# A decoder layer on one core: merge gates two ways, block sums in other buffers, and filler work placed by attention unit

## The chip, the core and the metric

The kernel runs on one core of one Trainium2 chip. A core has TensorE (PE, whose weight loads are listed as PEld), VectorE (DVE), ScalarE (ACT), GpSimd (POOL) and SyncE (SP), which here issues the transfers. Each engine works through its own list of instructions in order and waits at semaphores for the others. The metric is the device time of one execution in microseconds; every time in this document is in microseconds unless it is marked ns.

## What is computed

One layer with 1,024 tokens of 1,024 channels. The normed input is projected to everything that the three branches need, and to three merge gates of 1,024 channels each:

```python
xn = rms_norm(x, norm_mix)
proj = xn @ w_in        # NSA q, k/v, branch gates | conv GLU | memory q | 3 merge gates
br_nsa = nsa_attention(...) @ w_nsa_out    # compressed, selected, window; gated sum
br_conv = u @ w_conv_out                   # GLU, depthwise conv of 31 taps, LayerNorm, silu
br_mem = o_m @ w_mem_out                   # cross-attention into 256 memory tokens
gm = jax.nn.sigmoid(g_merge).reshape(b, s, N_BRANCH, D_MODEL)
merged = gm[:, :, 0] * br_nsa + gm[:, :, 1] * br_conv + gm[:, :, 2] * br_mem
h = x + merged @ w_out
hn = rms_norm(h, norm_ffn)
return h + (jax.nn.silu(hn @ w_gate) * (hn @ w_up)) @ w_down
```

## The kernel before

**Arithmetic.** All products keep float32 accuracy: each operand is split into a high part (a cast on ACT, `split`) and the low rest (a subtraction on DVE or POOL, `sub`), and `mm3` issues three matmuls, high by high, high by low and low by high. A matmul has 128 rows of weights and mostly 512 columns of tokens.

**Order of the program.** Norm and projections, the conv and memory branches and the attention's keys and values come first; then the attention, in 80 units (8 blocks of 128 queries, 2 groups, and for each a compressed unit, two selected and two window units); then the merge (branch projections, gated sums), the output projection, gate/up and down. A unit has a part `scores` (products, masks on DVE, exponentials on ACT, scales of the softmax on POOL in `softmax_tail`) and a part `values` (transposes, splits, products). `values` is issued LAG = 4 units behind its `scores`.

**The filler.** The merge gates are twelve pairs of 256 columns (`pairs`, in the order of the branches conv, memory, NSA). They depend on the normed input alone and are needed only in the merge, so they are put between other work: the instructions are written with a low priority (`low(FILL)`), and a scheduler, which picks the next instruction of each engine by priority among those that it deems ready, puts them into gaps. Their results go to one PSUM bank of their own (`fbank`, tile `pf`), their split weights to two buffers `fslab` (tile `fsl`), and they pass through DRAM (`zd`, `z1d`) to the merge.

A pair is 256 columns by 1,024 channels by 1,024 tokens, seen as two by two blocks. Before, all twelve go by seven half products in place of eight. Two of the seven use input blocks as they are (slabs 180 to 183 in the rows below): these are the *early* products, 24 matmuls a pair, with a load `fst` of 512 KB, a cast and a subtraction on POOL. The other five, 60 matmuls a pair, are the *late* products: four of them need sums of input blocks, of which three take the place of blocks in XN and one has slabs of its own, `T2`. So the block sums come behind the last early product that reads the old blocks. The sums use temporaries from `t4`, which the attention uses too. The late products need five weight operands, three of them with sums of weight blocks (`fs`, `wsx`, from a 512 KB load into the one buffer `wextra`): four sums on POOL, three of the five splits on POOL and two on DVE. Each result is added to a kept part on DVE (`put`, L882: tiles `fp`, `fz`). A list `spread` ties every late product to a point of the attention by an order-only dependency, in proportion to the work of the units.

**The merge** loads branch outputs and projection weights in 512 KB units, one weight unit for each two pairs' columns, reads the gates from `zd`, and multiplies.

Of the kernel before, what the change touches and what calls it, by code (L numbers as in the profile page):

```python
# [32 lines left out]
WB, LAG, SPREAD = 6, 4, 97  # L33
# [5 lines left out]
def hybrid_layer_kernel(  # L39
# [72 lines left out]
    def fbank(shape, dt=F32, p=P):  # L112
        return pfp.tile([p] + shape, dt, tag="pf", name=nm("pf"))
# [9 lines left out]
    class low:  # L123
        def __init__(self, by):
            self.by = by

        def __enter__(self):
            self.was = tc.cur_priority
            tc.cur_priority = self.was + self.by

# [125 lines left out]
    def unit(src, shape, alloc=wslab, eng=None, load=False):  # L256
# [4 lines left out]
        ld = nc.sync.dma_start(st, src)  # L261
        w = alloc([2] + shape)
        split(w[:, 0], w[:, 1], st, eng)
        return (w, ld.ins) if load else w

    def col_unit(w, c0, n=P, alloc=wslab, eng=None, load=False):
        return unit(w[:, c0:c0 + n].rearrange("(k p) c -> p k c", p=P), [w.shape[0] // P, n], alloc, eng,
                    load)
# [388 lines left out]
    with low(FILL):  # L657
        for n_, (b_, dp) in enumerate(pairs):
            w = col_unit(w_in, C_GM + b_ * D + 2 * dp * P, alloc=fslab, eng=nc.gpsimd)
            ps = fbank([512])  # L660
            for u in range(2):
                for k in range(4 * u, 4 * u + 4):
                    mm3(ps, w[:, 0, k, :], w[:, 1, k, :], xn(0, k, 0), xn(1, k, 0), k == 0, k % 4 == 3, True)
                z = fzp.tile([P, 512], F32, tag="fz", name=nm("fz"))
                nc.scalar.copy(z, ps)
                nc.sync.dma_start(zd[b_, 2 * dp, :, 0:512] if u else z1d[n_], z)

    T2 = [slab([2, 2, 512]) for _ in range(2)]
    for j in range(2):
        x11, x12, x22 = XN[0][j], XN[1][j], XN[1][2 + j]  # L670
        f = []
        for t in (x11, x12, x22):
            f.append(t4([2, 512]))
            nc.gpsimd.tensor_tensor(f[-1], t[:, 0].bitcast(F32), t[:, 1].bitcast(F32), op=OP.add)
        sub(nc.vector, f[1], f[1], f[0])
        split(x12[:, 0], x12[:, 1], f[1])
        sub(nc.vector, f[2], f[2], f[1])
        split(T2[j][:, 0], T2[j][:, 1], f[2])
    for sign, u in ((1, 0), (-1, 1)):
        for j in range(2):  # L680
            t, x_ = T2[j], XN[0][2 * u + j]
            d0, d1 = t4([2, 512]), t4([2, 512])
            for d, hl, eng in ((d0, 0, nc.vector), (d1, 1, nc.gpsimd)):
                a, b = (t, x_) if sign > 0 else (x_, t)
                sub(eng, d, a[:, hl].bitcast(F32), b[:, hl].bitcast(F32))
            nc.vector.tensor_tensor(d0, d0, d1, op=OP.add)
            split(x_[:, 0], x_[:, 1], d0)
# [79 lines left out]
    def values(u, tiles):  # L767
# [4 lines left out]
        if br == 0:  # L772
            b = bank([4, P], at=1)
            for h in range(4):
                nc.tensor.transpose(b[:64, h, :], tiles[h], ident)
            pt = t2([4, P], F32R)
            split(pt[:64], pt[64:], b[:64])
            m = mm(o.rearrange("p h q -> p (h q)"), vcmp[:, g, :], pt.rearrange("p h q -> p (h q)"), True, False)
            anchors.append((3, m.ins))
            return  # L780
# [18 lines left out]
        anchors.append((WB + nb, m.ins))  # L799
# [15 lines left out]
    load_q(0, 0)  # L815
    for u in units:
        if u[2] == 1 and u[3] == 1 and u[:2] != (NT - 1, 1):
# [4 lines left out]
    for u_ in ahead:  # L822
        values(*u_)


    late = len(pairs) * 20
    total = sum(w_ for w_, _ in anchors)
    spread, run = [], 0
    for w_, ins in anchors:
        run += w_  # L830
        while len(spread) < min(late, late * run * 100 // (total * SPREAD)):
            spread.append(ins)

    class fill_weights:
# [3 lines left out]
        def take(self, src, eng):  # L838
# [4 lines left out]
            split(w[:, 0], w[:, 1], src, eng)  # L843
            return w

    with low(FILL):
        fw, at_ = fill_weights(), [0]
        gp = nc.gpsimd

        def fill_product(ps, w, op, start):  # L850
            for k in range(4):
                first = mm3(ps, w[:, 0, k, :], w[:, 1, k, :], op(0, k), op(1, k), start and k == 0, k == 3, True)
                tc.add_manual_dep(first.ins, spread[at_[0]].name, ORDER, reason="spread over the attention")
                at_[0] += 1

        def blk(tiles):
            return lambda hl, k: tiles[k // 2][:, hl, k % 2, :]

        t1, t2_, t3_, t4_, x22 = blk(XN[1][:2]), blk(T2), blk(XN[0][:2]), blk(XN[0][2:]), blk(XN[1][2:])
        for n_, (b_, dp) in enumerate(pairs):  # L860
            r = wextra([2, KT, P], F32)
            for c in range(2):
                c0 = C_GM + b_ * D + (2 * dp + c) * P
                nc.sync.dma_start(r[:, c], w_in[:, c0:c0 + P].rearrange("(k p) c -> p k c", p=P))
            A11, A12, A21, A22 = r[:, 0, 0:4], r[:, 0, 4:8], r[:, 1, 0:4], r[:, 1, 4:8]
            sc = fzp.tile([P, 4, P], F32, tag="fz", name=nm("fs"))
            z1 = fzp.tile([P, 512], F32, tag="fz", name=nm("fz"))
            nc.sync.dma_start(z1, z1d[n_])
            pq = fstp.tile([P, 2, 512], F32, tag="fst", name=nm("fp"))
            p15, c12 = pq[:, 0], pq[:, 1]  # L870
            gp.tensor_tensor(sc, A21, A22, op=OP.add)
            s1 = fw.take(sc, gp)
            sub(gp, sc, sc, A11)
            sub(gp, A12, A12, sc)
            s4 = fw.take(A12, nc.vector)
            s2 = fw.take(sc, gp)
            sub(gp, A11, A11, A21)
            s3 = fw.take(A11, nc.vector)
            a22 = fw.take(A22, gp)

            def put(o, ps, z):
                nc.vector.tensor_tensor(o, ps, z, op=OP.add)  # L882

            ps = fbank([512])
            fill_product(ps, s1, t1, True)
            put(p15, ps, z1)
            fill_product(ps, s4, x22, False)
            put(c12, ps, z1)
            ps = fbank([512])
            fill_product(ps, s2, t2_, True)  # L890
            put(c12, ps, c12)
            nc.sync.dma_start(zd[b_, 2 * dp, :, 512:], c12)
            fill_product(ps, s3, t3_, False)
            put(p15, ps, p15)
            nc.sync.dma_start(zd[b_, 2 * dp + 1, :, 512:], p15)
            fill_product(ps, a22, t4_, False)
            put(z1, ps, z1)
            nc.sync.dma_start(zd[b_, 2 * dp + 1, :, 0:512], z1)
# [383 lines left out]
```

## Time and profile before

| | before |
|---|---|
| device time, median of 3 runs | 1787.79 |
| lowest and highest of the 3 | 1784.71, 1789.56 |
| the profiled execution's own time | 1791.22 |
| its span, first to last instruction | 1789.5 |
| PE busy | 1698.7 (95%) |
| DVE, ACT, POOL busy | 1146.3 (64%), 752.3 (42%), 747.3 (42%) |
| mean granted PE clock over the span | 0.981 |

Busy shares are of the whole span, which has stages with different limits. The granted clock is a share of the full TensorE clock, 2.4 GHz; 1.2 GHz would be 0.5, and a stretch between the two had some time at either level. The profiled execution is 3.43 above the median of the three runs; sums below are made in its time.

### The profile page before, as it was taken

Reading aid. Unit: us, or ns where it says so; the run is one execution under the profiler, and the core shown is the slowest. Engines: PE = TensorE matmul, PEld = TensorE weight load, DVE = VectorE, ACT = ScalarE, POOL = GpSimd, SP = SyncE. Lnnn points to the kernel's source line nnn. Section 1 sums busy time; section 2 is a strip of 40 time slices with the busy share of each in tenths; the row PEclk is TensorE's granted clock in tenths of the full one; section 3 lists DMA queues with packets and bytes.
Section 4 is the critical chain, followed back from the end, with each engine's and each line's share of the span. In section 5 each row is a group of like instructions: output and inputs, shape, how many; then the busy total and the mean of one; then the engine's idle time right before and its main releaser. Section 6 shows DMA issues by size and latency. Waiting matters only on the chain. (4 is left out here: it accounts for less than half of the span.)

```text
span 1789.5 us, 25276 instructions
## 1 busy us (share of the span) xinstructions
PE 1698.7 (95%) x9339; PEld 1467.7 (82%) x9339; DVE 1146.3 (64%) x1839; ACT 752.3 (42%) x1412; POOL 747.3 (42%) x605
## 2 busy tenths in 40 slices
PE   7999798999699999999779999999999999999999
PEld 5887787999588888998667899888888888888887
DVE  5499998766877788787343641775445455457665
ACT  5312444444476666766323432552222222224432
POOL 1102575575665555664222420055555776510000
PEclk9999899999799999999999999999999999999999
DMA  6212342222223222123635622233323444795663
GB/s 203 73 32 89 130 135 84 65 90 100 72 81 88 71 71 66 57 66 114 198 120 167 207 66 83 112 104 97 112 83 106 164 136 153 238 394 184 210 240 121
DMA packets 213463, 222.96 MB, mean 125 GB/s; under 512 B 28439, under 2 KB 157751, under 8 KB 212315
## 3 DMA queue, kind: packets, MB, share of 16 engines
q1 hardware_dynamic: 213338, 221.35, 38.0%
q8 instruction: 73, 1.20, 0.3%
q14 instruction: 52, 0.42, 0.1%
HBM read 165.73 MB, written 55.57 MB: 124 GB/s over the span
## 5 line engine op out<-in xcount | busy, mean ns | idle before, releaser
L151 PE MATMUL pf<-slab,fsl 128*128 128x512 f32 x1092 | 291.3, 407 | 28.3 <-ACT fsl L138 16.0
L151 PEld LDWEIGHTS pf<-slab,fsl 128*128 128x128 f32 x1092 | 202.7, 194 | 73.3 <-ACT fsl L138 19.0
L151 PE MATMUL ps<-slab,wsl 128*128 128x512 f32 (+1 forms) x1068 | 239.3, 381 | 3.0 <-DVE t L135 2.4
L151 PEld LDWEIGHTS ps<-slab,wsl 128*128 128x128 f32 x1068 | 194.0, 189 | 41.9 <-issue 2.6
L377 DVE SCALAR_TENSOR_TENSOR slab<-slab,cw 128x1019 f32<-128x1019 f32 (+18 forms) x120 | 188.6, 1581 | 1.8
L151 PE MATMUL ps<-wsl,slab 128*128 128x256 f32 x1224 | 165.1, 288 | 3.3 <-POOL wsl L135 1.6
L1112 DVE TENSOR_TENSOR t<-ps,t 128x512 f32<-128x512 f32 x127 | 86.9, 688 | 115.1 <-PE ps L151 114.0
L151 PEld LDWEIGHTS ps<-wsl,slab 128*128 128x128 f32 x1224 | 156.0, 195 | 5.6 <-POOL wsl L135 1.9
L151 PE MATMUL ps<-slab,fsl 128*128 128x512 f32 x636 | 147.7, 389 | 0.0
L151 PEld LDWEIGHTS ps<-slab,fsl 128*128 128x128 f32 x636 | 119.4, 188 | 24.8
L151 PE MATMUL ps<-slab,wsx 128*128 128x512 f32 (+1 forms) x596 | 136.5, 383 | 0.2 <-ACT wsx L138 0.2
L135 DVE TENSOR_TENSOR t<-ps,t 128x512 fp32r<-128x512 f32 (+3 forms) x196 | 121.1, 630 | 21.6 <-ACT t L138 20.1
L151 PEld LDWEIGHTS ps<-slab,wsx 128*128 128x128 f32 x596 | 109.5, 188 | 22.5 <-ACT wsx L138 0.6
L151 PE MATMUL ps<-t,slab 128*128 128x256 f32 x624 | 120.1, 298 | 2.4 <-DVE t L135 2.0
L138 ACT CAST t<-ps 128x512 fp32r<-128x512 f32 (+2 forms) x192 | 98.0, 540 | 48.5 <-PE ps L791 44.2
L151 PEld LDWEIGHTS ps<-t,slab 128*128 128x128 f32 x624 | 96.1, 194 | 10.3 <-DVE t L135 3.2
L151 PE MATMUL ps<-slab,qt 128*128 128x384 f32 (+3 forms) x384 | 100.5, 353 | 3.6 <-DVE sm L759 3.3
L1125 POOL TENSOR_TENSOR t<-t,t 128x512 f32<-128x512 f32 x21 | 39.2, 1865 | 116.9 <-DVE t L1112 42.4
L1077 POOL TENSOR_TENSOR t<-st 128x512 f32<-128x512 f32 x21 | 27.4, 1303 | 139.6 <-DVE slab L135 112.6
L929 POOL TENSOR_TENSOR slab<-slab,t 128x512 f32<-128x512 f32 x32 | 44.0, 1392 | 93.0 <-DVE t L928 87.3
L1216 PE MATMUL ps<-wsl 128*128 128x512 f32 x336 | 81.2, 389 | 0.0
L1216 PE MATMUL ps<-fsl 128*128 128x512 f32 x330 | 79.8, 389 | 0.0
(264 smaller groups left out, 3381.1 us busy)
## 6 DMA issues: line engine op xcount, KB each, us to landing
t<-in_w_down_dram SPq DMA_DIRECT2D x70, 256.0 KB, 3.9
wsx<-in_w_in_dram SPq DMA_DIRECT2D x24, 512.0 KB, 5.1
t<-zd SPq DMA_DIRECT2D x24, 512.0 KB, 4.1
st<-in_w_in_dram SPq DMA_DIRECT2D x22, 512.0 KB, 3.7
st<-in_w_gate_dram SPq DMA_DIRECT2D x22, 512.0 KB, 4.0
st<-in_w_up_dram SPq DMA_DIRECT2D x22, 512.0 KB, 4.0
ad<-t SPq DMA_DIRECT2D x44, 256.0 KB, 2.9
ads<-slab SPq DMA_DIRECT2D x33, 256.0 KB, 2.9
```

The lines of the kernel that those rows point to most:

```text
L135: eng.tensor_tensor(o, a, b, op=OP.subtract)
L138: nc.scalar.copy(hi, src)
L151: m = nc.tensor.matmul(o, a, b, start=start, stop=stop, skip_group_check=chain)
L377: return nc.vector.scalar_tensor_tensor(acc[:, s:], u[:, :S - s], cw[:, ct, 30 - s:31 - s], acc[:, s:], op0=OP.mult, op1=OP.add)
L929: nc.gpsimd.tensor_tensor(a, a, z, op=OP.add)
L1077: gp.tensor_tensor(s12[:, 0], u[:, 0], u[:, 1], op=OP.add)
L1112: nc.vector.tensor_tensor(o, a_, b_, op=OP.add)
L1125: nc.gpsimd.tensor_tensor(u4, u4, c22, op=OP.mult)
L1216: nc.tensor.matmul(B[t], a_, b_, start=start and k == 0 and j == 0, stop=k == FH - 1 and j == 2, skip_group_check=True)
```

## The change

The first two pairs (N_PLAIN = 2) are computed plainly: eight half products of 12 matmuls, all of them early, in four groups, with two `fst` loads a pair; the other ten stay with seven. The early products of the last four pairs (N_DUE = 4) are written at normal priority. The block sums are restated as `block_sub`: two differences (high on DVE, low on POOL), an addition on DVE, a cast on ACT and a subtraction on DVE, eight times; their temporaries come from `wextra` (four) and from `fslab` (four), in place of `t4`. All five weight splits of a late pair are on POOL. Late products get the priority of the attention unit that they are due with (`at(steps[...])`), spread over the units FILL_FROM = 4 to FILL_TO = 82 by weight, and each pair's weights that of eight units earlier (FILL_LEAD); the order-only dependency is now to the `values` of the unit LAG before.

```diff
-WB, LAG, SPREAD = 6, 4, 97
+WB, LAG = 6, 4
+FILL_LEAD, FILL_FROM, FILL_TO = 8, 4, 82
+N_PLAIN, N_DUE = 2, 4
...
-    with low(FILL):
-        for n_, (b_, dp) in enumerate(pairs):
-            w = col_unit(w_in, C_GM + b_ * D + 2 * dp * P, alloc=fslab, eng=nc.gpsimd)
-            ps = fbank([512])
-            for u in range(2):
...
+    for n_ in range(NP):
+        with low(FILL if n_ < NP - N_DUE else 0):
+            for c in range(2 if n_ < N_PLAIN else 1):
+                st = fstp.tile([P, KT, P], F32, tag="fst", name=nm("fst"))
+                nc.sync.dma_start(st, gate_columns(n_, c))
+                w = fslab([2, KT, P])
+                split(w[:, 0], w[:, 1], st, gp)
+                for half in range(2 if n_ < N_PLAIN else 1):
+                    ps = fbank([512])
+                    for u in range(2):
+                        half_product(ps, w[:, :, 4 * u:4 * u + 4], blk((x12, x22)[u] if half else (x11, x21)[u]), u == 0)
+                        if u or n_ >= N_PLAIN:
+                            z = f512("fz")
+                            nc.scalar.copy(z, ps)
+                            nc.sync.dma_start(gate_out(n_, c, half) if u else z1d[n_], z)
...
+    def block_sub(o, a, b, temps):
+        d = temps([2, 2, 512], F32)
+        for hl, eng in ((0, nc.vector), (1, gp)):
+            sub(eng, d[:, hl], a[:, hl].bitcast(F32), b[:, hl].bitcast(F32))
+        nc.vector.tensor_tensor(d[:, 0], d[:, 0], d[:, 1], op=OP.add)
+        split(o[:, 0], o[:, 1], d[:, 0])
+
     for j in range(2):
...
-            f.append(t4([2, 512]))
-            nc.gpsimd.tensor_tensor(f[-1], t[:, 0].bitcast(F32), t[:, 1].bitcast(F32), op=OP.add)
...
+        block_sub(x12[j], x12[j], x11[j], wextra)
+        block_sub(T2[j], x22[j], x12[j], wextra)
+    for j in range(2):
+        block_sub(x11[j], T2[j], x11[j], fslab)
+    for j in range(2):
+        block_sub(x21[j], x21[j], T2[j], fslab)
...
-        while len(spread) < min(late, late * run * 100 // (total * SPREAD)):
-            spread.append(ins)
...
-            s4 = fw.take(A12, nc.vector)
...
-            s3 = fw.take(A11, nc.vector)
...
+        while len(due) < (NP - N_PLAIN) * 20 * run // total:
+            due.append(k_)
...
+        with at(step_of(j_, -FILL_LEAD)):
+            r = wextra([2, KT, P], F32)
...
+                u_ = due[j_ + 4 * q + k]
+                with at(steps[min(u_ + 1, len(steps) - 1)]):
+                    m = mm3(ps, ws[q][:, 0, k, :], ws[q][:, 1, k, :], op(0, k), op(1, k), start and k == 0, k == 3, True)
+                    if u_ >= LAG:
+                        tc.add_manual_dep(m.ins, anchors[u_ - LAG].name, ORDER, reason="spread over the attention")
```

**Instructions in all.** On PE the filler has 24 matmuls of 128x512 more (1,116 in place of 1,092 with `slab` and `fsl` operands). DVE has 30 fewer (the 24 subtractions of late weights gone, 10 fewer `put`, 4 more of 128x1024 in the block sums), POOL 6 more (18 more late weight splits, 8 fewer weight sums, 2 more early splits, 4 fewer others of the late weights, 2 fewer in the block sums), SP 6 fewer.

**PE at the start of the attention.** In rows of the order a name is tile<-weights,moving operand, then the shape and the count; `pf` rows are filler, those with slabs 180 to 183 early products, `identr` rows the transposes of the last keys, `L716` (now `L752`) the first queries, `kcmp` rows the scores of a compressed unit, `L791` (now `L827`) transposes of `values`. Before:

```order
L151 MATMUL pf_4159<-slab_180,fsl_4156 128x512 x6
L151 MATMUL pf_4159<-slab_181,fsl_4156 128x512 x6
L637 MATMUL ps_3746<-identr,t_471_3670 128x128 x4
L151 MATMUL pf_4159<-slab_182,fsl_4156 128x512 x6
L151 MATMUL pf_4159<-slab_183,fsl_4156 128x512 x6
L637 MATMUL ps_3752<-identr,t_479_3741 128x128 x4
L716 MATMUL ps_4247<-ident,t_558_4244 128x128 x4
L151 MATMUL ps_4257<-kcmp,qt_4252 128x64
```

All early products are over when the attention's first scores begin. After the change, at the same place:

```order
L164 MATMUL pf_4115<-slab_183,fsl_4112 128x512 x6
L649 MATMUL ps_3752<-identr,t_479_3741 128x128 x4
L752 MATMUL ps_4415<-ident,t_566_4412 128x128 x4
L164 MATMUL pf_4151<-slab_180,fsl_4148 128x512 x6
L164 MATMUL pf_4151<-slab_181,fsl_4148 128x512 x6
L164 MATMUL ps_4425<-kcmp,qt_4420 128x64
```

Six early pairs more (pf_4151, pf_4187, pf_4223, pf_4259, pf_4295, pf_4331, 144 matmuls) now stand between the scores and values of the first sixteen units. The last of them, and what follows to the first late product (pf_8294):

```order
L164 MATMUL pf_4331<-slab_182,fsl_4328 128x512 x6
L164 MATMUL pf_4331<-slab_183,fsl_4328 128x512 x6
L164 MATMUL ps_4811<-t_711_4917,slab_3169 128x256
L164 MATMUL ps_4931<-slab_3166,qt_4855 128x256 x2
L164 MATMUL ps_4811<-t_711_4917,slab_3169 128x256 x3
L827 MATMUL ps_4945<-ident,wsl_4821 128x128 x4
L164 MATMUL ps_4936<-slab_3166,qt_4855 128x256 x2
L164 MATMUL ps_4966<-slab_3167,qt_4855 128x256 x2
L164 MATMUL ps_4811<-t_719_4946,slab_3169 128x256
L811 MATMUL ps_4981<-ident,t_699_4869 64x128 x4
L164 MATMUL ps_4811<-t_719_4946,slab_3169 128x256 x3
L164 MATMUL ps_4971<-slab_3167,qt_4855 128x256 x2
```

Between the last early product and the first late one there is now attention work alone.

**DVE in that stretch.** `fsl_4394` and `fsl_4400` are temporaries of block sums (L148 the subtractions, L713 the addition, `slab_180` to `slab_183` the blocks), `t_711` and `t_719` the splits of the attention's transposed probabilities that the PE rows above read, `L795` the masks of the scores. After the change:

```order
L148 TENSOR_TENSOR t_711_4917<-ps_4916,t_711_4917 128x512
L713 TENSOR_TENSOR fsl_4394<-fsl_4394 128x1024
L732 RECIPROCAL sm_4878<-sm_4859 128x4
L795 ISA wsl_4896,sm_4897<-ps_4899,strip 128x256
L795 ISA sm_4897 128x1
L795 ISA wsl_4896,sm_4897<-ps_4904,strip 128x256
L148 TENSOR_TENSOR fsl_4400<-slab_182,slab_4362 128x1024
L148 TENSOR_TENSOR slab_181<-fsl_4394,slab_181 128x1024
L148 TENSOR_TENSOR t_719_4946<-ps_4945,t_719_4946 128x512
L713 TENSOR_TENSOR fsl_4400<-fsl_4400 128x1024
```

The block sums of the first two slabs of XN stand between the splits of the attention's units; before, they stood ahead of the attention.

**PE behind the attention.** `wsl` and `wsx` rows are the merge's first and second weight unit, `pf` rows filler (slabs 321 to 324 are the rewritten blocks). Before:

```order
L151 MATMUL ps_9270<-slab_9245,wsl_9250 128x512 x3
L151 MATMUL pf_8994<-slab_182,fsl_8962 128x512
L151 MATMUL pf_8994<-slab_183,fsl_8962 128x512 x6
L151 MATMUL pf_9061<-slab_321,fsl_9045 128x512 x6
L151 MATMUL pf_9061<-slab_322,fsl_9045 128x512 x6
L151 MATMUL pf_9061<-slab_323,fsl_9045 128x512 x6
L151 MATMUL pf_9061<-slab_324,fsl_9045 128x512 x6
L151 MATMUL pf_9088<-slab_4190,fsl_9052 128x512 x6
L151 MATMUL pf_9088<-slab_4191,fsl_9052 128x512 x6
```

This block goes on with pf_9088 and pf_9154; then six matmuls of the second weight unit (wsx_9317) follow, and 36 filler matmuls of pf_9181 behind them. After the change:

```order
L164 MATMUL ps_9251<-slab_9226,wsl_9231 128x512 x3
L164 MATMUL ps_9304<-slab_9211,wsx_9298 128x512 x2
L164 MATMUL ps_9318<-slab_9211,wsx_9298 128x512 x2
L164 MATMUL ps_9304<-slab_9211,wsx_9298 128x512
L164 MATMUL ps_9304<-slab_9216,wsx_9298 128x512 x3
L164 MATMUL ps_9304<-slab_9221,wsx_9298 128x512 x3
L164 MATMUL pf_9162<-slab_4362,fsl_9124 128x512 x6
L164 MATMUL pf_9162<-slab_4363,fsl_9124 128x512 x6
```

The merge's second weight unit follows the first directly, and 48 late matmuls of the last pair stand in pieces of 12 among merge rows, in place of the block.

## Rows read from the trace of the kernel before

**Rows 1.** The page's first part (busy, share of the span, instructions) and its slices of 44.7 us each: PE's busy tenths, its granted clock in tenths, and GB/s moved.

```profile
PE 1698.7 (95%) x9339; PEld 1467.7 (82%) x9339; DVE 1146.3 (64%) x1839; ACT 752.3 (42%) x1412; POOL 747.3 (42%) x605
...
PE   7999798999699999999779999999999999999999
...
PEclk9999899999799999999999999999999999999999
...
GB/s 203 73 32 89 130 135 84 65 90 100 72 81 88 71 71 66 57 66 114 198 120 167 207 66 83 112 104 97 112 83 106 164 136 153 238 394 184 210 240 121
```

**Rows 2.** Windows, a row for each: its length, then busy time and instructions of PE, PEld, DVE, ACT and POOL, granted PE clock, DMA share, GB/s. The last one is a stretch of the gate/up stage in which every matmul is of 128x512.

```profile
300.00:400.00 100.00, 96.10 (x690) 89.56 (x689) 67.97 (x86) 45.82 (x92) 61.24 (x39) 0.98 0.28 88
400.00:500.00 100.00, 85.22 (x547) 75.91 (x548) 71.62 (x134) 48.34 (x113) 56.99 (x51) 0.88 0.25 81
500.00:850.00 350.00, 340.15 (x2153) 304.56 (x2152) 271.21 (x811) 234.79 (x580) 204.30 (x236) 0.99 0.27 78
850.00:950.00 100.00, 79.67 (x340) 62.71 (x339) 36.36 (x47) 29.14 (x34) 19.04 (x14) 0.93 0.53 167
...
1200.00:1300.00 100.00, 100.00 (x443) 82.81 (x442) 53.08 (x60) 30.59 (x40) 61.09 (x42) 1.00 0.35 111
```

**Rows 3.** The same for the two stretches around the attention's ends.

```profile
450.00:492.00 42.00, 28.30 (x135) 23.20 (x134) 34.66 (x64) 21.29 (x52) 25.32 (x23) 0.72 0.27 76
...
853.00:927.00 74.00, 53.67 (x217) 40.88 (x216) 22.09 (x29) 19.92 (x25) 19.04 (x14) 0.91 0.44 139
```

**Rows 4.** Timeline of PE at the attention's start: start, duration, operation, count, and in brackets the idle time before it and what ended that.

```profile
454.07 2.91 PE L151 MATMUL pf<-slab,fsl 128*128 128x512 f32 x12
...
463.57 0.72 PE L637 MATMUL ps<-identr,t 128*128 128x128 f32 x4 [2.89 <-DVE t L135]
465.46 4.94 PE L151 MATMUL pf<-slab,fsl 128*128 128x512 f32 x12 [1.17 <-ACT fz L665]
475.73 0.75 PE L637 MATMUL ps<-identr,t 128*128 128x128 f32 x4 [5.33 <-DVE t L135]
...
484.48 1.12 PE L151 MATMUL ps<-slab,qt 128*128 128x128 f32 x4 [2.41 <-DVE sm L759]
...
490.19 0.95 PE L151 MATMUL pf<-slab,fsl 128*128 128x512 f32 x3
```

**Rows 5.** Timeline of PE behind the attention, in the same form.

```profile
853.15 3.00 PE L151 MATMUL pf<-slab,fsl 128*128 128x512 f32 x12
...
869.26 1.75 PE L151 MATMUL pf<-slab,fsl 128*128 128x512 f32 x7
878.36 5.28 PE L151 MATMUL pf<-slab,fsl 128*128 128x512 f32 x12 [7.36 <-ACT fsl L138]
884.92 3.01 PE L151 MATMUL pf<-slab,fsl 128*128 128x512 f32 x12 [1.28 <-DVE fp L882]
...
906.50 4.90 PE L151 MATMUL pf<-slab,fsl 128*128 128x512 f32 x12 [7.02 <-ACT fsl L138]
...
927.33 2.88 PE L151 MATMUL ps<-slab,fsl 128*128 128x512 f32 x12
...
969.94 3.02 PE L151 MATMUL pf<-slab,fsl 128*128 128x512 f32 x12 [1.65 <-DVE fp L882]
```

**Rows 6.** PE's waits (who waits for whom: total, times, longest), in 860 to 927 (first two rows), in 500 to 853 (the third, the largest of that stretch), in 300 to 400 (the last).

```profile
PE pf L151 <- ACT fsl L138: 16.0, 3, 7.4
PE pf L151 <- DVE fp L882: 3.8, 4, 1.3
...
PE ps L791 <- DVE t L135: 3.4, 3, 2.2
...
PE pf L151 <- ACT fz L665: 3.9, 3, 2.5
```

**Rows 7.** Timeline of DVE, and below it of POOL, during block sums.

```profile
454.47 3.04 DVE L135 TENSOR_TENSOR slab<-t,slab 128x1024 fp32r<-128x1024 f32 x1
457.55 1.23 DVE L135 TENSOR_TENSOR t<-slab,slab 128x1024 f32<-128x1024 f32 x1
467.74 3.40 DVE L135 TENSOR_TENSOR t<-slab,slab 128x1024 f32<-128x1024 f32 x1
...
454.03 2.40 POOL L135 TENSOR_TENSOR t<-slab,slab 128x1024 f32<-128x1024 f32 x1 [4.11 <-DVE slab L135]
466.76 3.29 POOL L135 TENSOR_TENSOR t<-slab,slab 128x1024 f32<-128x1024 f32 x1 [3.62 <-DVE t L686]
```

**Rows 8.** Groups of instructions by line and shape in the attention (500 to 850): count, busy, mean ns; and what ended idle time before them.

```profile
L135 POOL TENSOR_TENSOR fsl<-fs,fsl 128x512 fp32r<-128x512 f32 x18 | 24.2, 1343 | 5.9 <-ACT fsl L138 5.1 <-DMA t<-qd 0.9
L135 POOL TENSOR_TENSOR fsl<-wsx,fsl 128x512 fp32r<-128x512 f32 x10 | 13.8, 1380 | 7.0 <-ACT fsl L138 7.0
L135 POOL TENSOR_TENSOR fs<-fs,wsx 128x512 f32<-128x512 f32 x9 | 11.6, 1292 | 0.5
...
L135 DVE TENSOR_TENSOR fsl<-wsx,fsl 128x512 fp32r<-128x512 f32 x18 | 19.3, 1070 | 0.2
```

**Rows 9.** The early weights (tile fst): cast and subtraction, with shortest, median and longest ns; and transfers from issue to landing.

```profile
L138 ACT CAST fsl<-fst x12: 1045/1052/1097, 21.1 to 425.7; 128x1024 fp32r<-128x1024 f32 x12
L135 POOL TENSOR_TENSOR fsl<-fst,fsl x12: 2371/2410/3377, 22.2 to 426.9; 128x1024 fp32r<-128x1024 f32 x12
...
DMA to landing us min/median/max: 3.6/3.7/6.4
```

More of the change, by code (lines that the diff above doesn't have):

```diff
@@ L253, in norm_x, with unit @@
                   js)
-    def unit(src, shape, alloc=wslab, eng=None, load=False):
+    def unit(src, shape, alloc=wslab, eng=None):
         if alloc is fslab:
@@ new lines, in hybrid_layer_kernel, with gate_columns, gate_out, half_product @@
+    gp = nc.gpsimd
+    def gate_columns(n_, c):
+        c0 = C_GM + pairs[n_][0] * D + (2 * pairs[n_][1] + c) * P
+        return w_in[:, c0:c0 + P].rearrange("(k p) c -> p k c", p=P)
+    def gate_out(n_, c, half):
+        return zd[pairs[n_][0], 2 * pairs[n_][1] + c, :, half * 512:(half + 1) * 512]
+    def half_product(ps, w, op, start):
+        return [mm3(ps, w[:, 0, k, :], w[:, 1, k, :], op(0, k), op(1, k), start and k == 0, k == 3, True)
+                for k in range(4)]
+    def blk(tiles):
+        return lambda hl, k: tiles[k // 2][:, hl, k % 2, :]
@@ L822, in hybrid_layer_kernel @@
     for u_ in ahead:
+        steps.append(tc.cur_priority)
         values(*u_)
[L826 to L830, printed above, removed]
-        while len(spread) < min(late, late * run * 100 // (total * SPREAD)):
-            spread.append(ins)
     class fill_weights:
@@ L842, in take, with step_of @@
             self.n += 1
-            split(w[:, 0], w[:, 1], src, eng)
+            split(w[:, 0], w[:, 1], src, gp)
             return w
[L846 to L860, printed above, removed]
+    fw = fill_weights()
+    weight = [WB + u[0] + 1 - (max(0, u[0] - 4) if u[2] == 2 else 0) if u[2] else 3 for u in units]
+    weight += [weight[-1]] * LAG
+    total, run, due = sum(weight[FILL_FROM:FILL_TO]), 0, []
+    for k_ in range(FILL_FROM, FILL_TO):
+        run += weight[k_]
+        while len(due) < (NP - N_PLAIN) * 20 * run // total:
+            due.append(k_)
+    def step_of(j, shift):
+        return steps[min(max(due[min(j, len(due) - 1)] + shift, 0), len(steps) - 1)]
+    for n_ in range(N_PLAIN, NP):
+        j_ = 20 * (n_ - N_PLAIN)
+        with at(step_of(j_, -FILL_LEAD)):
             r = wextra([2, KT, P], F32)
             for c in range(2):
-                c0 = C_GM + b_ * D + (2 * dp + c) * P
-                nc.sync.dma_start(r[:, c], w_in[:, c0:c0 + P].rearrange("(k p) c -> p k c", p=P))
+                nc.sync.dma_start(r[:, c], gate_columns(n_, c))
             A11, A12, A21, A22 = r[:, 0, 0:4], r[:, 0, 4:8], r[:, 1, 0:4], r[:, 1, 4:8]
             sc = fzp.tile([P, 4, P], F32, tag="fz", name=nm("fs"))
-            z1 = fzp.tile([P, 512], F32, tag="fz", name=nm("fz"))
+            z1 = f512("fz")
             nc.sync.dma_start(z1, z1d[n_])
```

94 lines of the change are left out of this document (45 added, 49 removed).

## The prediction, made before the changed kernel was run

> **What bounds the kernel now.** The first part of the page is read first: PE is busy for 1698.7 of 1789.5, so no other engine bounds the whole, and there are 90.8 of PE's time that are not busy [rows 1]. The slices say where they lie: PE's row falls to 6 in the slice of 447 to 492 and to 7 in the two of 850 to 939; it is 7 also in the first and in that of 179 to 224, and 8 or 9 everywhere else [rows 1]. A slice is an average, so windows come next: 400 to 500 is busy for 85.22 with a granted clock of 0.88, 850 to 950 for 79.67 at 0.93, while the attention between them, 500 to 850, is busy for 340.15 of 350 at 0.99 [rows 2]. So the attention itself has 10 to give at most; the two stretches at its ends have 35 idle between them, and more by the clock. A stretch of the gate/up stage gives the price of a matmul of 128x512 when nothing waits: 100.00 / 443 = 0.2257 [rows 2]. I use that below, and not the mean durations of single records, which overlap.
>
> The timeline then names the waits. At the attention's start, PE waits for the block sums and keys on DVE (2.89, 5.33) and for masks (2.41), and twelve filler matmuls take 4.94 in place of about 2.9 [rows 4]. Behind the attention, the filler that did not fit stands as one block, and PE waits in it twice for the cast of a weight operand, 7.36 and 7.02, and several times about 1 for the single result bank [rows 5]: 16.0 on casts and 3.8 on the bank [rows 6]. Nothing of the merge is done meanwhile, since PE's list is in order.
>
> **The change part by part.**
>
> *Arithmetic.* Two pairs lose the seventh's saving: 24 matmuls more, 24 x 0.2257 = **+5.4**. They run while PE is busy, so all of it counts.
>
> *The block behind the attention.* Work in 853.15 to 927.33: 120 filler matmuls, 84 of the merge of 512 columns, ten of 256 columns (all counted in the timeline, of which [rows 5] has the ends and the waits); 204 x 0.2257 + 10 x 0.12 = 47.2. The stretch takes 74.18 [rows 5], so 27.0 are lost, of which 74.00 - 53.67 = 20.3 are idle [rows 3], two rows of twelve at 5.28 and 4.90 cost 4.2 more than at full clock [rows 5], and the rest is the granted clock of 0.91 [rows 3]. Another wait for the bank, 1.65 at 970 [rows 5], brings the loss to 28.6. The 120 matmuls do not vanish; they move into the attention, where in PE's new order pieces of twelve stand between units, and only 48 late ones remain among merge rows. After the change what can be left here is a wait for the result bank at some of these four pieces, about 1 each [rows 5]: 3, bounds 1 to 9, the upper one with a wait of 7 for a merge weight as there was for filler weights. So **-26**, bounds -20 to -28. What hides the weights now is the attention: they are written eight units ahead, and a unit is about (853 - 484) / 80 = 4.6 long [rows 4, 5], so there are 37 for a load, four sums, a cast and five splits.
>
> *The attention's start.* Before, 450 to 492 has 13.7 idle, and a granted clock of 0.72 says that 2 x 0.28 x 42 = 23.5 of it were at the lower level of 1.2 GHz [rows 3]. If the idle time lies inside those, 9.8 busy were at half speed and 4.9 of them are lost; if it lies outside, 11.7. So 18.6 to 25.4 are lost here; I take 24, as the rows of the first units, last of all the 4.94, are slow [rows 4]. After the change the first four block sums need none of the old blocks that early products still read, the other four come sixteen units later, and 144 early matmuls (32.5 of PE) stand between the first units. They fill just these waits. Left are single waits for the chain of the first four sums: 8, bounds 3 to 14.
>
> But what is late next is the second set of four sums. They overwrite slabs 180 to 183, so they start behind the last early product, one buffer of their temporaries comes free only then, and the late products cannot start before they are done. In the order no filler stands in between; the attention matmuls there are 7,168 columns, 7168 / 512 x 0.2257 = 3.2, or 4.3 with their short ones. One block sum costs on DVE 1.23 (half, alone), an addition and a low part of the same shape = 3.7, with a cast of 1.05 on ACT [rows 7, 9]: four take 14.8 on DVE at least, interleaved with masks and splits, and POOL halves of 2.40 to 3.29 [rows 7] stand ahead of the softmax scales. The splits t_711, t_719 queue behind them, and PE waits for these splits. With 14.8, some 6 of the attention's own DVE work (an estimate from DVE's 271.21 in 350 [rows 2], over the 8 that PE's part would take with filler), less 4.3 of PE: 16 idle, 1 by the clock: 17. Bounds: 14.8 less 4.3, 10; and 24 if half of the halves are as long as 3.04 to 3.40 [rows 7]. The stretch at the start in all: 8 + 17 - 24 = **+1**, bounds -12 to +13.
>
> *Early section.* With plain pairs the group of 24 is not cut by an evacuation: of the 3.9 that PE waited for casts of results (fz) in 300 to 400 [rows 6] 2 go. Nine more filler matmuls stand ahead of the gap that the slice of 179 to 224 shows [rows 1]: 9 x 0.2257 = 2. So **-4**, bounds -5 to 0.
>
> *At nothing.* Two transfers `fst` more, 3.7 each, and 2 POOL splits of 2.41 [rows 9] are hidden by POOL's and SP's idle time early (POOL 61.24 of 100 [rows 2]); were they not, one product would come 6 later. DVE loses 24 splits of late weights, 1.07 each [rows 8]: off the path, since in the attention PE waits for DVE only 3.4 in its largest row [rows 6]. POOL gains per pair two splits, 2 x 1.38 = 2.8 on top of 3 x 1.36 + 4 x 1.29 = 9.2 [rows 8]; ten pairs, 120 in place of about 83 in 500 to 850, which lifts POOL from 204 to some 241 of 350 [rows 2]. Covered by the lag of four units, 4 x 4.6 = 18; if that cover is gone, see the slower rival.
>
> *Sum* in the profiled execution's time: 1791.2 + 5.4 - 26 + 1 - 4 = 1767.6. That execution lies 3.4 above the median of the runs, so the forecast for the median is 1764, rounded up to **1765** as the clock's part is the weakest. Bounds together: 1791.2 + 5.4 - 28 - 12 - 5 - 3.4 = 1748 and 1791.2 + 5.4 - 20 + 13 - 0 - 3.4 = 1786.
>
> **The rivals.**
>
> *Two-engine lock at the block sums.* Each of the eight sums begins a DVE and a POOL half together, both with two inputs in SBUF. In the row at 454.47 the DVE instruction took 3.04 where the same kind took 1.23 alone, and it began 0.44 after a POOL one of 2.40 and ended 1.08 after that one's end; likewise 3.40 beside 3.29 [rows 7]. The price is 2 for each sum, so 8 more on DVE in the second set, and as much in the first, where early matmuls cover half: 12 on top, 1777. Against it: half of my 17 is already taken from such waits. Chance 0.17. The Trainium skill, "SBUF — State Buffer", section "Who interferes with whom", says that VectorE with two SBUF inputs and a reading GpSimd use one shared interface and that one holds it while the other waits in full; the trace agrees (3.04 = 1.96 of waiting + 1.08). By that rule the eight sums are done one engine after the other, and the sum would be 1777; by the row of 1.23 alone it is 1765.
>
> *The merge is bound by its loads.* The block of filler hid loads: 853 to 927 moved 139 GB/s for 74 [rows 3]. Without it the same 10.3 MB come in about 50, which is 206 GB/s. Against it, the merge's own slice of 984 to 1029 moved 207 and a later one 394, with PE at 9 in both [rows 1]. If half of the gain is given back, 1778. Chance 0.08.
>
> *The change doesn't do what it says.* Late products are placed in the attention, but their weights, now all split on POOL behind softmax scales, come late, and PE stands before them there as it did behind the attention (7 each): 3 or 4 of these and the gain is gone, 1787. For it, the casts of late weights are what PE waits for now [rows 6]; against it, these waits come only where there is no attention work between, and in 500 to 850 before there is none. Chance 0.08.
>
> *Slower.* POOL's work on a pair comes in runs of five or six instructions, about 8 long, ahead of the scales of a unit's softmax. `values` of that unit wait for the scales, and PE stands. The unit has 18 from its scores to its values, but its own chain of masks, exponentials and scales takes a large part of them in the late units with 8 blocks. If a run of 8 is too long by 3.3, ten pairs cost 33 and the time is 1798; it decides from 2.8 a pair on, since 28.2 lie between 1765 and 1793.2. Against it, POOL had 9.2 for each pair before, in runs of up to 6, and the largest group of waits in the attention is 3.4 in all, on DVE [rows 6]. Chance 0.09.
>
> **How the numbers follow.** The forecast has 0.58. A measurement of this kernel tells 0.3%, 5.4, from no change: faster is under 1782.4, slower over 1793.2. The lock ends under 1782 in most cases (0.15 of 0.17) and the load rival in all: faster 0.58 + 0.15 + 0.08 = 0.81; same 0.08 + 0.02 = 0.10; slower 0.09. The range leaves out the slower rival and what lies past the bounds: 1749 to 1787.
>
> **What would show it.** In the profile after: no idle of 7 in a block of pf rows behind the attention, and the merge's second weight unit directly behind the first; 850 to 950 busy for over 95 (shifted by the gain). At the start, a clock above 0.9 in the window in which the first scores lie; some 50 to 60 later a dip of 10 to 24 of PE's idle time, with waits of `ps` on the splits `t` of DVE, just behind the last early product. PE's matmul count 24 up. The prediction is wrong if that dip is 30 and more, if PE waits for softmax scales on POOL inside the attention, or if late products wait for their weights there.

## The result, and the profile after

The changed kernel takes 1768.43 (median of 4 runs, 1768.1 to 1771.8) against 1788.01 of the kernel before (4 runs): a ratio of 0.9897, interval 0.9879 to 0.9916. The forecast was 1765, within 1749 to 1787. The medians lie 19.6 apart and the forecast wanted 22.8; the spans of the two profiled executions lie 23.1 apart, because the one before was 3.2 above the median of these runs and the one after is 0.3 below. Sums by stretch, below, are of these two executions. The profiled execution took 1768.1 with a span of 1766.4. Its page, to be read beside [rows 1]:

```profile
PE 1694.7 (96%) x9363; PEld 1469.5 (83%) x9363; DVE 1119.2 (63%) x1809; ACT 748.1 (42%) x1408; POOL 749.5 (42%) x611
...
PE   6999799998897999999999999999999999999999
...
PEclk9999899999998999999999999999999999999999
```

PE has 24 matmuls more, and the two slices of 7 behind the attention are gone; a 7 has come at 530 to 574, where before there was a 9. The windows, in the form of [rows 2]:

```profile
400.00:500.00 100.00, 86.69 (x548) 76.97 (x547) 49.51 (x107) 43.36 (x97) 51.52 (x38) 0.91 0.35 110
500.00:600.00 100.00, 87.90 (x497) 75.03 (x495) 74.62 (x217) 65.47 (x191) 75.88 (x88) 0.90 0.26 77
...
850.00:950.00 100.00, 98.60 (x504) 84.02 (x503) 60.08 (x93) 53.54 (x72) 27.14 (x23) 1.00 0.65 221
950.00:1050.00 100.00, 100.00 (x539) 87.02 (x538) 46.63 (x60) 35.89 (x52) 41.54 (x31) 1.00 0.37 124
```

850 to 950 is busy for 98.60 where it was 79.67 [rows 2], with loads at 221 GB/s, so the merge is not bound by them. In 860 to 927 PE waited 16.0 for casts of filler weights [rows 6]; its waits in 850 to 1000 are now one row, for a cast of a merge weight. Below it stand those of 500 to 550:

```profile
PE ps L164 <- ACT wsl L151: 1.3, 1, 1.3
...
PE ps L827 <- POOL wsl L737: 4.3, 1, 4.3
PE ps L164 <- DVE sm L795: 3.2, 3, 2.5
PE ps L164 <- DVE sm L767: 1.4, 1, 1.4
```

To say where the time went I take PE's loss by stretch: the length less the columns of the matmuls that start there, each counted once, at 0.2257 for 512. (Short matmuls cost more than their columns, so a loss is not all idle time; it is for comparing kernels.)

| stretch | loss before | loss after | difference |
|---|---|---|---|
| 200 to 400 | 40.3 | 36.0 | -4.3 |
| 400 to 450 | 5.5 | 11.7 | +6.2 |
| 450 to 492 | 26.5 | 15.8 | -10.7 |
| 492 to 600 | 24.3 | 36.2 | +11.9 |
| 600 to 800 | 34.3 | 33.5 | -0.8 |
| 800 to 927 | 40.4 | 14.1 | -26.3 |
| 927 to 1100 | 8.4 | 4.9 | -3.5 |
| 1100 to 1400 | 13.2 | 11.8 | -1.4 |

Together -28.9, and +5.4 for the added matmuls: -23.5, against -23.1 between the spans. The 11.9 are the dip that was forecast: 525 to 552, around the end of the last early product, where the loss is 18.1 after 6.3. (Two expectations below give this loss as 16 or 16.4, from a count that took some matmuls twice.) The window of the dip, before and after, in the form of [rows 2]:

```profile
525.00:552.00 27.00, 25.21 (x158) 22.22 (x157) 20.43 (x63) 17.93 (x50) 16.26 (x23) 1.00 0.31 89
525.00:552.00 27.00, 17.25 (x79) 13.40 (x78) 26.72 (x50) 14.23 (x37) 22.38 (x18) 0.71 0.19 55
```

PE is idle for 9.8 of it after 1.8, and the granted clock fell from 1.00 to 0.71: 2 x 0.29 x 27 = 15.7 were at the lower level of 1.2 GHz. PE's timeline there:

```profile
533.54 0.50 PE L164 MATMUL ps<-slab,qt 128*128 128x256 f32 x2 [1.43 <-DVE sm L767]
...
537.74 1.22 PE L164 MATMUL ps<-slab,qt 128*128 128x256 f32 x4 [2.53 <-DVE sm L795]
...
548.07 0.48 PE L827 MATMUL ps<-ident,wsl 128*128 128x128 f32 x1 [4.31 <-POOL wsl L737]
...
550.26 1.05 PE L164 MATMUL pf<-slab,fsl 128*128 128x512 f32 x2
```

and those of DVE and, below, POOL:

```profile
529.53 3.38 DVE L148 TENSOR_TENSOR fsl<-slab,slab 128x1024 f32<-128x1024 f32 x1
...
534.02 3.26 DVE L713 TENSOR_TENSOR fsl<-fsl 128x1024 f32<-128x1024 f32 x1
537.96 1.22 DVE L148 TENSOR_TENSOR fsl<-slab,slab 128x1024 f32<-128x1024 f32 x1
...
529.44 2.40 POOL L148 TENSOR_TENSOR fsl<-slab,slab 128x1024 f32<-128x1024 f32 x1 [1.35 <-DVE slab L148]
533.85 2.35 POOL L148 TENSOR_TENSOR fsl<-slab,slab 128x1024 f32<-128x1024 f32 x1
537.47 3.51 POOL L737 TENSOR_SCALAR t<-t,sm,gsb 128x64 f32<-128x64 f32 x4 [1.28 <-DVE sm L732]
543.18 3.33 POOL L148 TENSOR_TENSOR fsl<-slab,slab 128x1024 f32<-128x1024 f32 x1
546.50 2.05 POOL L737 TENSOR_SCALAR wsl<-wsl,sm,gsb 128x256 f32<-128x256 f32 x2
```

DVE's half from 529.53 and its addition from 534.02 take 3.38 and 3.26 beside a POOL half, and a half of the same shape takes 1.22 without one. The scales of a softmax wait on POOL behind a half of 3.33, and PE's 4.31 ends when the first of the two scales is done.

### The profile page after: what moved, and what is told of

Same layout as the page of the kernel before. It is cut to its first block, busy times and chain, and to the rows that moved or that the text cites. A ratio compares the mean times of both kernels' runs of the same rounds, so it can differ in the third digit from the quotient of the medians.

```text
span 1766.4 us, 25275 instructions
## 1 busy us (share of the span) xinstructions
PE 1694.7 (96%) x9363; PEld 1469.5 (83%) x9363; DVE 1119.2 (63%) x1809; ACT 748.1 (42%) x1408; POOL 749.5 (42%) x611
## 5 line engine op out<-in xcount | busy, mean ns | idle before, releaser
L164 PE MATMUL pf<-slab,fsl 128*128 128x512 f32 x1116 | 287.0, 403 | 6.0 <-ACT fz L704 6.0
L164 PEld LDWEIGHTS pf<-slab,fsl 128*128 128x128 f32 x1116 | 207.1, 192 | 47.9 <-ACT fz L704 8.3
L148 DVE TENSOR_TENSOR t<-ps,t 128x512 fp32r<-128x512 f32 (+3 forms) x196 | 120.4, 631 | 27.3 <-ACT t L151 26.2
L164 PE MATMUL ps<-t,slab 128*128 128x256 f32 x624 | 116.3, 297 | 2.3 <-DVE t L148 1.2
L164 PE MATMUL ps<-slab,qt 128*128 128x384 f32 (+3 forms) x384 | 95.8, 349 | 6.4 <-DVE sm L795 4.9
L148 POOL TENSOR_TENSOR wsl<-st,wsl 128x1024 fp32r<-128x1024 f32 x13 | 36.6, 2815 | 107.2 <-ACT wsl L151 107.0
```

The source lines that it names most:

```text
L148: eng.tensor_tensor(o, a, b, op=OP.subtract)
L164: m = nc.tensor.matmul(o, a, b, start=start, stop=stop, skip_group_check=chain)
```

## The experiments

The runs of the kernel before that were made beside these have medians of 1788.2, 1789.2 and 1789.4, so a difference of about 1 between runs of two series says nothing. Two questions were put: which part of the change gives the gain, and what the new block sums cost. N_DUE is 4 in every run with the new sums and 0 in every run with the old ones; no run changes it by itself.

All diffs are against the changed kernel unless a sentence says otherwise.

**Plain pairs alone.** The kernel before with two plain pairs, which is the changed kernel with its other parts undone:

```diff
-N_PLAIN, N_DUE = 2, 4
+N_PLAIN, N_DUE = 2, 0
...
-        block_sub(x12[j], x12[j], x11[j], wextra)
...
+            f.append(t4([2, 512]))
+            nc.gpsimd.tensor_tensor(f[-1], t[:, 0].bitcast(F32), t[:, 1].bitcast(F32), op=OP.add)
...
-                with at(steps[min(u_ + 1, len(steps) - 1)]):
+                with low(FILL):
...
-            ws.append(fw.take(A12))
+            ws.append(fw.take(A12, nc.vector))
```

> The kernel before with two pairs plain and nothing else: old block sums with t4 temporaries, late products at low priority along the old spread list, two splits on DVE. Ten pairs' late work in place of twelve. Theory A (the block of filler behind the attention is gone because there is less late work, whatever places it): no block behind the attention, waits of pf rows there under 5 in all, 24 matmuls more: 1788 - 27 + 5.4, a start as before or up to 8 worse: 1763 to 1774. Theory B (the placement by unit is what removes the block): the block stays with its two waits of 7, and the time is 1785 to 1794.

1761.12 (ratio 0.9847, 0.983 to 0.9863): nearest to theory A, 2 below its range. No placement is needed to clear most of the block (loss in 800 to 1100: 30.6 after 48.8; waits of `pf` rows of 7.2 in 850 to 1000, where A wanted under 5), and this one part beats the whole change. What A did not expect is the start: the loss in 200 to 492 falls from 72.3 to 52.9, and 492 to 600 takes back 5.2 of that.

**Placement alone**, with the old sums and two splits on DVE as above:

```diff
-N_PLAIN, N_DUE = 2, 4
+N_PLAIN, N_DUE = 0, 0
```

> The kernel before with the placement by attention unit alone: all twelve pairs by seven products, old block sums, two splits on DVE, early products at low priority. Theory A (less late work decides): about 60 late matmuls still stand as a block behind the attention and PE waits in it once or twice for a weight cast of 7: a gain of 8 to 16, 1772 to 1780. Theory B (placement decides): the whole of the gain behind the attention without the 24 matmuls: 1758 to 1764.

1772.76 (0.9912, 0.9884 to 0.994), the four runs between 1766.7 and 1777.9. In between, as theory A has it; PE still waits 5.2 once for a weight cast in 850 to 1000.

**Both**, with the old sums and two splits on DVE as above:

```diff
-N_PLAIN, N_DUE = 2, 4
+N_PLAIN, N_DUE = 2, 0
```

> Both, two plain pairs and the placement by unit, with the old block sums (three sums of t4 temporaries on POOL ahead, then DVE) and two late splits on DVE. Against the changed kernel this takes back the new form of the sums, their buffers and the three moved splits. My prediction's part on the start (the new sums move the stall but do not make it smaller: +1) wants 1764 to 1772, with a loss of PE at the start of the attention and no dip later. If the new sums help the start by 10 or more, this is 1776 or above; if they cost (the measured dip of 16 at 525 to 552 is their price in full), it is 1755 to 1760.

1749.31 (0.9782, 0.9767 to 0.9797): 19.1 faster than the changed kernel and below all three forecasts. The new sums and the moved splits (with N_DUE) cost more than the whole dip. Its losses are 4.2 in 400 to 450, 14.2 in 450 to 492 and 30.0 in 492 to 600, where the changed kernel has 11.7, 15.8 and 36.2. Timeline of POOL and DVE there: the sums' first part

```profile
350.19 4.76 POOL L714 TENSOR_TENSOR t<-slab 128x1024 f32<-128x1024 f32 x2
364.76 5.75 POOL L714 TENSOR_TENSOR t<-slab 128x1024 f32<-128x1024 f32 x2
...
440.38 2.35 DVE L148 TENSOR_TENSOR slab<-t,slab 128x1024 fp32r<-128x1024 f32 x2
```

is done in 350 to 380, the first blocks are rewritten at 440 and the last at 516.23. In the changed kernel the first half starts at 457.76 on DVE and the last block is rewritten at 551.64.

**Halves on DVE.** The changed kernel with

```diff
-        for hl, eng in ((0, nc.vector), (1, gp)):
+        for hl, eng in ((0, nc.vector), (1, nc.vector)):
```

> The changed kernel with both halves of each block sum on DVE, none on POOL: nothing holds POOL's scales up and no two engines share an operand read. If the lock between DVE and POOL makes the dip (DVE instructions of 3.3 where 1.2 is usual, POOL scales behind halves of 2.4 to 3.4), the loss of 16.4 in the 27 us of the dip falls by 5 to 9 and the time is 1759 to 1764. If DVE's own amount of work makes it, four halves more of 1.22 stand ahead of masks and splits and the time is 1771 to 1774. If it is neither, 1767 to 1769.

1762.46 (0.9856, 0.9841 to 0.9871): 6.0 faster, though DVE does eight instructions more. So the POOL halves cost 6.0. Two things went with them, the lock with DVE and their place ahead of POOL's scales, and the run does not tell one from the other. The gain does not lie where it was expected: the loss in 525 to 552 falls only from 18.1 to 16.4, not by 5 to 9, and 3.1 come from 450 to 492, where the first sums are. In 500 to 560 PE's longest wait on POOL's scales is down from 4.3 (those for `t`, not shown, are 2.3 where they were 0.3):

```profile
PE ps L827 <- POOL wsl L737: 1.5, 1, 1.5
PE ps L164 <- DVE sm L795: 1.4, 3, 0.8
```

**Other buffers.** The changed kernel with

```diff
-        d = temps([2, 2, 512], F32)
+        d = [t4([2, 512]), t4([2, 512])]
```

> The changed kernel with the temporaries of the eight block sums in t4 tiles again, in place of wextra and fslab; the new form of the sums and all splits on POOL stay. It lies 19 above the run with the old sums and two splits on DVE (1768.4 against 1749.3), and three things differ: the buffers, the form, the splits. Theory buffers (wextra is held by key and value weights to 457, fslab by the last early product to 521, so the sums come late): the sums can start earlier, the dip at 525 to 552 goes, 1749 to 1755. Theory form or splits: 1764 to 1770.

1773.20 (0.9917, 0.9902 to 0.9932). The theory of the buffers falls: taking them back makes it worse. Only the first of the eight sums starts early (349.71); the second reads the block that the first rewrites, and that ends at 459.9.

**Splits on DVE:**

```diff
-            ws.append(fw.take(A12))
+            ws.append(fw.take(A12, nc.vector))
...
-            ws.append(fw.take(A11))
+            ws.append(fw.take(A11, nc.vector))
```

> The changed kernel with the splits of S3 and S4 of each late pair on DVE as before (20 in all), the rest as changed. Theory buffers: the dip and the waits of 400 to 500 stay, 1765 to 1770. Theory splits (POOL work in the attention costs PE waits): 1755 to 1762. My prediction's slower rival (POOL's runs of 8 us cost 2.8 or more a pair) would want 1740 or less.

1765.03 (0.9872, 0.9858 to 0.9887): about 3.4 for ten pairs, 0.3 a pair, with all four runs below all four of the changed kernel. The two splits that were moved to POOL cost a tenth of what the slower rival needed.

**Old sums, splits on POOL.** Only `block_sub` and N_DUE are undone:

```diff
-N_PLAIN, N_DUE = 2, 4
+N_PLAIN, N_DUE = 2, 0
...
-        block_sub(x12[j], x12[j], x11[j], wextra)
...
+        sub(nc.vector, f[1], f[1], f[0])
+        split(b_[:, 0], b_[:, 1], f[1])
+        sub(nc.vector, f[2], f[2], f[1])
+        split(T2[j][:, 0], T2[j][:, 1], f[2])
```

> The changed kernel with the old block sums in t4 (form and buffers) and N_DUE = 0; all five late splits on POOL stay. Theory buffers or form: 1748 to 1753, no different from the run with two splits on DVE (1749.3) by more than 3. Theory splits: 1757 or above.

1751.11 (0.9795, 0.978 to 0.981): 1.8 above the run with two splits on DVE, and 22.1 below the one with t4 temporaries and the new form. With buffers and splits equal, the 22 are the form of the sums and N_DUE together. Against the changed kernel it is 17.3 faster; of the 15.4 between the two spans 7.2 lie in 400 to 450, 2.4 in 450 to 492 and 4.8 in 492 to 600.

**T2 from the difference.** The run with t4 temporaries, with

```diff
+        return d
...
-        block_sub(x12[j], x12[j], x11[j], wextra)
-        block_sub(T2[j], x22[j], x12[j], wextra)
+        d0, d1 = block_sub(x12[j], x12[j], x11[j], wextra)
+        sub(nc.vector, d1, x22[j][:, 0].bitcast(F32), d0)
+        nc.vector.tensor_tensor(d1, d1, x22[j][:, 1].bitcast(F32), op=OP.add)
+        split(T2[j][:, 0], T2[j][:, 1], d1)
```

> The run with t4 temporaries and the new form of the sums (1773.2), with one dependency gone: T2 is made from the float32 difference x12 - x11 that is still in its temporary, not from the block x12 after that was rewritten. Rewriting x12 has to wait for the last key and value products that read it (457 in the changed kernel); the difference does not. Theory dependency: DVE and POOL make the first four sums early, in 350 to 440, and the time is 1749 to 1756, that of the old sums with the splits on POOL (1751.1). Theory work (the new form has more DVE instructions at the start): 1768 to 1774.

1770.25 (0.9899, 0.9882 to 0.9915). The arithmetic of the first four sums now lies in 351 to 374, as the theory of the dependency says, and the loss in 525 to 552 is 10.4, near the 10.3 of the run with t4 temporaries (18.1 in the changed kernel), but the time hardly falls: PE lost 40.5 in 200 to 400, where that run lost 36.9, with 3.1 for a scale of the memory attention, in the stretch where DVE now does eight instructions of the sums (that these delay it is inferred), and the chain on SP, shown further down, stays. So the theory of the work has the time (1768 to 1774), and the theory of the dependency is right only on when the sums are made. The edit also takes two halves off POOL, so it is not the dependency alone.

**Late products as before**, with their weights and stores, at low priority along the old list:

```diff
-                with at(steps[min(u_ + 1, len(steps) - 1)]):
+                with low(FILL):
...
+                    tc.add_manual_dep(m.ins, spread[j_ + 4 * q + k].name, ORDER, reason="spread over the attention")
```

> The changed kernel with its late products placed as before (low priority, the old spread list); plain pairs, new sums and splits stay. With the old sums this placement costs 11.8 (1761.1 against 1749.3). In the order 100 late matmuls stand as a block behind the attention again. Theory supply (the two weight buffers set how many late pairs fit into the attention; ten fit with the old placement and early sums, and late sums leave less room): the block is back with one or two waits of 7, 1778 to 1786. Theory additive: 1780. If the placement matters only with twelve late pairs: 1767 to 1770.

1796.15 (1.0037, 1.0024 to 1.005), slower than the kernel before and above all three forecasts. The block is back, in 850 to 1000 with one of the old waits for a cast and seven for the result bank:

```profile
PE pf L164 <- ACT fsl L151: 7.0, 1, 7.0
PE pf L164 <- DVE fp L916: 6.7, 7, 1.6
```

**No plain pair:**

```diff
-N_PLAIN, N_DUE = 2, 4
+N_PLAIN, N_DUE = 0, 4
```

> The changed kernel with no pair plain: 24 matmuls fewer (-5.4), twelve late pairs. With the old sums two plain pairs are worth 23.4 under this placement (1772.8 against 1749.3). Prediction's own terms (plain costs 5.4 and its early matmuls fill the start): the early products end at the attention's start, so the second set of sums lies there and not at 525, and 84 late matmuls stand behind the attention: 1775 to 1788. If plain pairs are only a cost: 1760 to 1763.

1797.03 (1.0051, 1.0033 to 1.007), 9 above the upper forecast. The loss is 30.3 in 800 to 927 (14.1 in the changed kernel) and 43.2 in 200 to 400 (36.0).

**One plain pair, old sums** (against the run with both):

```diff
-N_PLAIN, N_DUE = 2, 0
+N_PLAIN, N_DUE = 1, 0
```

> The run with old sums, splits on DVE and placement by unit (1749.3), with one plain pair in place of two: 12 matmuls fewer, eleven late pairs. In the order the last late pair ends shortly behind the attention. Theory supply: the eleventh pair just fits, 1744 to 1750. Theory additive (half of the 23.4 between none and two): 1759 to 1763.

1754.12 (0.9808, 0.9792 to 0.9824). Twelve matmuls fewer, and still 4.8 slower than with two (1751.0 to 1756.6 against 1747.3 to 1751.1): nearer to the two than half way, so most of the gain comes with the first pair.

**Fastest with its last halves on DVE** (against the run with both):

```diff
-            for d, hl, eng in ((d0, 0, nc.vector), (d1, 1, nc.gpsimd)):
+            for d, hl, eng in ((d0, 0, nc.vector), (d1, 1, nc.vector)):
```

> The fastest so far (old sums, two plain pairs, placement by unit, two splits on DVE; 1749.3) with the four POOL halves of its last block sums on DVE. If the lock of DVE and POOL costs there too (DVE rows of 3.27, 2.41 and 4.76 for two, beside POOL ones of 2.4), 1744 to 1748. If DVE's amount of work counts (four halves more, 4.9), 1751 to 1754. Neither: 1748 to 1751.

1748.51 (0.9779, 0.9762 to 0.9795), no different from 1749.31. With these sums, four halves on POOL rather than DVE cost nothing that can be measured. These two are the fastest kernels here, 1.1% under the changed one.

## Why the prediction was right, and where its steps were not

The time, the sign and the place of each large term came out, but that the total came out too is in part luck: two errors of opposite sign cancelled, and one cause was put in the wrong place.

| term | forecast | measured |
|---|---|---|
| block behind the attention | -26 | -29.8 (800 to 1100) |
| start of the attention | +1 | +7.4 (400 to 600) |
| early section | -4 | -4.3 (200 to 400) |
| 600 to 800 | none | -0.8 |
| 1100 to 1400 | none | -1.4 |
| 24 matmuls | +5.4 | +5.4 |

**The block.** The mechanism held and the size nearly: no wait for filler weights is left there. But I wrote that what hides the weights now is the attention, by the placement eight units ahead. The four combinations with the old sums say what does: neither 1788.2, plain pairs 1761.1, placement 1772.8, both 1749.3. With the new sums each of the two is worth 28 (1796.2 and 1797.0 against 1768.4). So the plain pairs were mis-sized most: I booked them as 24 matmuls, +5.4, and they bring 23 to 29 net. A plain pair has no late matmuls, where a pair by seven has 60 with five split operands; it has 96 early ones in place of 24, with two loads and two splits, and these lie where PE was waiting: with plain pairs alone the loss is 19.4 lower in 200 to 492 and 18.2 lower in 800 to 1100. The new sums with their buffers cost 17.3 in all. The forecast had their dip at 17, but ahead of it a gain of 16 that it laid in part to their new form; plain pairs bring that gain without them (the loss in 450 to 492 is 13.9 with plain pairs alone, 15.8 in the changed kernel).

**The start.** I wanted the loss in 450 to 492 to fall by 16, from 24 to 8; it fell by 10.7, and the granted clock rose from 0.72 to 0.88 there, where I had named 0.9 as the sign. In 400 to 450, where I had booked nothing, 6.2 were lost. The step that failed there is the one booked at nothing: that the loads `fst` are hidden by SP's idle time. SP was not idle but waiting, in order. The chain in the changed kernel, from the timelines of SP, ACT, DVE, POOL and PE:

```profile
400.16 0.36 SPq L589 DMA_DIRECT2D qd<-slab  x1
400.57 0.57 SPq L705 DMA_DIRECT2D zd<-fz  x1
401.24 1.12 SPq L695 DMA_DIRECT2D fst<-in_w_in_dram  x1
...
407.68 1.05 ACT L151 CAST fsl<-fst 128x1024 fp32r<-128x1024 f32 x1 [9.57 <-DMA fst<-in_w_in_dram]
...
409.11 1.09 ACT L631 ACTIVATE t<-ps 128x512 f32<-128x512 f32 x2
...
409.74 6.56 DVE L633 RECIPROCAL t<-t 128x512 f32<-128x512 f32 x2 [9.60 <-ACT t L631]
...
413.17 10.07 POOL L635 TENSOR_TENSOR slab<-slab,t 128x512 f32<-128x512 f32 x8 [1.97 <-DVE t L633]
...
425.42 0.51 PE L649 MATMUL ps<-identr,t 128*128 128x128 f32 x4 [2.51 <-DVE t L148]
...
429.30 2.90 PE L164 MATMUL ps<-wsx,slab 128*128 128x256 f32 x12 [3.37 <-DVE slab L148]
```

SP stands 15.0 before the store of queries (L589), whose slab DVE had not finished; the gate's store and the load `fst` are behind it. ACT's cast waits for that load, the LayerNorm's square root behind the cast, then DVE, POOL and in the end PE. The run with plain pairs, placement and old sums has the load ahead of that store:

```profile
391.96 0.33 SPq L705 DMA_DIRECT2D zd<-fz  x1
394.44 0.37 SPq L695 DMA_DIRECT2D fst<-in_w_in_dram  x1
401.18 0.36 SPq L589 DMA_DIRECT2D qd<-slab  x1
...
402.07 6.57 DVE L633 RECIPROCAL t<-t 128x512 f32<-128x512 f32 x2 [0.93 <-ACT t L631]
```

The reciprocal begins 7.7 sooner, and PE has no wait in 400 to 450. The waits of about 2.5 and 3.4 are in all six kernels that have both plain pairs and the new sums, and in none of the eight others, the kernel before among them: it takes both to put that load behind that store. (N_DUE is 4 in these six as well; but the changed kernel written with N_DUE = 0 has the load behind the store too, and the one with old sums written with N_DUE = 4 has it ahead.)

**The dip.** Forecast 17 (10 to 24), of which 16 idle and 1 by the clock, with PE waiting for splits `t` behind block sums on DVE. It came in the forecast place, at 11.8 above the loss of the kernel before in 525 to 552. Of these 8.0 are idle time; the other 3.8, an estimate from the loss less the idle time of the two windows, go with the granted clock of 0.71, so the clock was mis-sized too. The releasers differ: I had named splits, and it was masks on DVE (1.43, 2.53) and scales on POOL (4.31), which I had listed as a sign against the forecast. My sum counted DVE's work and had half of the 17 from the lock; the run with all halves on DVE is 6.0 faster, where the rival wanted 12 on top, and those 6.0 need not be the lock alone. The rule of the Trainium skill that I weighed ("SBUF — State Buffer", "Who interferes with whom") agrees with the trace: 3.38 is what is left of the POOL half when DVE starts, 2.31, and 1.07 of its own.

**The rivals.** The loads did not bind the merge (221 GB/s at 98.60 of 100). Late products did not wait for weights in 500 to 850. The splits moved to POOL cost 0.3 a pair, not 2.8.

**What stays open** is how the 19 of the new sums divide. Their form and buffers make 17.3 (the run with old sums and all splits on POOL; N_DUE differs too, but in the changed kernel it alone moves only one short stretch of PE's order). With t4 temporaries the form makes 22.1, less surely, as N_DUE alone shifts PE's order through the attention there. The POOL halves are 6.0 of it in the changed kernel. But the dependency of T2 gave back only 2.9 when it was taken away, the buffers of the change gain 4.8 rather than cost, and the order on SP was not tried by itself: that its chain costs the 5.9 of the two waits, or the 7.2 of the loss in 400 to 450, is read from traces and not shown by a run.

## What to carry to other kernels

Count what it takes to feed a filler, and not its matmuls alone: here two plain pairs with more matmuls and fewer split operands gained more than a better place for the same work. When a change has several parts, a total that comes out as forecast says little of the parts; four combinations of two of them showed a cost of 19 that the total hid. Before booking a transfer at nothing, look at what stands ahead of it in the issuing queue and at which engine will wait in order for its landing.

## What the runs showed of the hardware

The lock between DVE and POOL reaches POOL's one-tensor scales too. Four of them (128x64) took 1.50 at 514.48, 0.39 each. The four from 537.47 took 3.51: two of them 0.39, and the two that met DVE instructions with two inputs in SBUF, begun at 537.96 and 539.10, took 1.43 and 1.36. The Trainium skill, in the section cited above, states this for a GpSimd instruction that reads SBUF; here it more than doubles a softmax's scales on the way to PE.
